# A hybrid encoder step on one core: squares and their parts issued earlier, values transposed once, the last attention units and a norm moved between weight pieces

## The chip, the core and the metric

The kernel runs on one core of one Trainium2 chip. The metric is the device time of one execution in microseconds (us). The kernel before was timed three times: 1239.25, 1239.58 and 1239.84 us, with the median at 1239.58. One execution was also recorded with the hardware profiler; all rows shown in this document are from such recordings.

## The reference

One layer of a streaming encoder works on 320 rows of width 2048 (256 of a new stream, 64 of a running one), in float32. What is computed, cut to what matters:

```python
z = rmsnorm(x, ln_g) @ w_in             # 2048 -> 1024 q, 128 k, 128 v, 1024 u, 1024 v_gate
q, k = rmsnorm(q, q_g), rmsnorm(k, k_g)  # per head of 64; 16 query heads, 2 key heads
a = sink_attention(q, k, v, bias, sinks) # chunks of 64 queries see up to 192 keys
s = gelu(u) * (W_s @ rmsnorm(gelu(v_gate)) + b)   # chunks of 128, chunk-causal
x = x + concat(rmsnorm(a), rmsnorm(s)) @ w_out
y = x + relu(rmsnorm(x) @ w_up)**2 @ w_down       # 2048 -> 8192 -> 2048
```

New keys, new values and the normalised gate rows of the running stream are returned too.

## The kernel before

All activations are held transposed: features lie on the partitions, and the 320 rows run along the free dimension. Every float32 weight is split into a rounded part and a remainder (`w_hi` on ScalarE, L115; `w_lo` on VectorE, L116), the activations likewise, and each product is the sum of three matmuls, hi times hi, hi times lo and lo times hi (L141). Weights come by the SP queue in pieces of 512 KB. A **piece** is four k-tiles by 256 output columns and gives 24 matmuls of 320 columns; a product over 2048 has four pieces. Three buffers each hold `w_hi` and `w_lo`, so a piece can be split while TensorE is up to three pieces behind.

The order of the products is: queries 0 together with keys and values in a first loop of twelve small steps (L237), which runs while x itself arrives; queries 1, 2 and 3; four products of the gate's v; four of u; then w_out, w_up and w_down. The first loop's steps append to `steps` the instructions that split that step's weights. x is normalised after the product: its squares (L288) are added up (L290 to L292), split into two parts (`two_parts`, L177 and L178), summed over the partitions by two matmuls with a constant matrix (L186, L187), and a reciprocal root `rx` is iterated on VectorE (L190 to L196). The evictions of the products multiply by `rx`.

Small matmuls are put between the pieces: `between_pieces` names, for each piece, a function to call when that piece has been issued; `narrow` is the list of such matmuls, and the next piece is ordered behind its last entry. What is put there: the norms (`rstd`), the sums of the queries' squares (`norm_q`, L323, whose result takes a way over ScalarE, two DMAs on the POOL queue, VectorE and POOL), the values' transposes (`values`, L349: six transposes in six windows of the 320 rows, copied by VectorE at L354), and the attention. `attend(i)` is a pipeline over ten units: it transposes the probabilities of unit i-2 into two PSUM banks called `misc` (L472), computes the scores of unit i (L420), and multiplies the transposed probabilities of unit i-3 with the values (L485); then come the softmax of unit i, the eviction of the attention output (L495, L497), and the copies of the transposed probabilities out of the two `misc` banks (L501). There are two `misc` banks in all, and `norm_q`, `rstd` and the row norm of the gate (`rows_norm`, L166 to L171) take one each for a while.

A scheduler decides at build time in which order the instructions stand on each engine; `issue_after(ins)` puts instructions of the block that are on the engine of `ins` behind it, and binds no other engine.

Of the kernel before, what the change touches and what calls it, by code (L numbers as in the profile page):

```python
# [15 lines left out]
P = 128  # L16
T = 320
# [3 lines left out]
KT = DM // P  # L21
# [9 lines left out]
def hymba_step_kernel(ctx: ExitStack, tc: tile.TileContext, i, o):  # L31
# [16 lines left out]
    def score_bank(p, name="s_ps"):  # L48
        return ps_sc.tile([P, 512], F32, name=f"{name}{p}", tag=f"s{p}")
# [50 lines left out]
    nc.vector.memset(hone[HD:P, 1:2], 1.0)  # L100


    loads, between, rests, steps, narrow, carry = [], [], [], [], [], []

    def load(out, in_):

# [15 lines left out]
    def products(w, k0, nk, c0, ps, rh, rl, deep=None, between_pieces={}, halves_behind={}):  # L122

        wv = w.rearrange("(kt p) n -> p kt n", p=P)
        behind = carry.pop() if carry else None
        steps.clear()
        for a in range(0, nk, 4):
            raw = (deep or wp).tile([P, 4, 256], F32, name="w_raw", tag="w_raw")  # L130
            hi, lo = w_tiles()
            load(raw, wv[:, k0 + a:k0 + a + 4, c0:c0 + 256])
            with tc.issue_after(halves_behind[a // 4]()) if a // 4 in halves_behind else nullcontext():
                high, low = halves(raw, hi, lo)
            tail = isinstance(ps, list) and a + 4 == nk
            for k, g in [(k, g) for g in range(2) for k in range(4)] if tail else [(k, g) for k in range(4) for g in range(2)]:
                kk = a + k
                for x, (w_, r_) in enumerate(((hi, rh), (hi, rl), (lo, rh))):
                    out = ps[g][:, 0:T] if isinstance(ps, list) else ps[:, g, 0:T]
                    with tc.issue_after(behind) if behind else nullcontext():  # L140
                        mm = nc.tensor.matmul(out=out, lhsT=w_[:, k, g * P:(g + 1) * P], rhs=r_(kk),  # L141
                                              start=(kk == 0 and x == 0), stop=(kk == nk - 1 and x == 2))
            steps.append((high, low, mm.ins))
            if a // 4 in between_pieces:
                with tc.issue_after(mm.ins):
                    between_pieces[a // 4]()
                    behind = narrow[-1]
                if a + 4 == nk:
                    carry.append(behind)
# [24 lines left out]
    def two_parts(acc):  # L174
        hl = sm.tile([P, 2, T], F32R, name="n_hl", tag="w2", bufs=4)
        hi, lo = hl[:, 0], hl[:, 1]
        nc.scalar.activation(out=hi, in_=acc, func=AF.Copy)  # L177
        rests.append(nc.vector.tensor_tensor(out=lo, in0=acc, in1=hi.bitcast(F32), op=ALU.subtract).ins)  # L178
        return hi, lo

    def rstd(acc, mean, eps, out):

# [101 lines left out]
    ssq2 = sm.tile([P, 2, T], F32, name="ssq2", tag="w2", bufs=4)  # L284
    for k in range(0, KT, 2):
        sq = sm.tile([P, 2, T], F32, name="sq2", tag="w2", bufs=4) if k else ssq2
        with tc.issue_after(steps[min(8 + k // 2, 11)][0]):
            nc.scalar.activation(out=sq, in_=xT[:, k:k + 2], func=AF.Square)  # L288
        if k:
            nc.vector.tensor_tensor(out=ssq2, in0=ssq2, in1=sq, op=ALU.add)  # L290
    ssq = sums("ssq")
    nc.vector.tensor_tensor(out=ssq, in0=ssq2[:, 0], in1=ssq2[:, 1], op=ALU.add)  # L292

    kv = sm.tile([P, 2, T], F32, name="kv", tag="w2", bufs=4)
    with tc.issue_after(steps[-1][0]):
        nc.scalar.activation(out=kv, in_=kv_ps[:, :, 0:T], func=AF.Copy)
    rk, rx = rstd_b("rk"), rstd_b("rx")

# [2 lines left out]
    def evict_q(g, q_ps):  # L301
        qg = qT[:, :, 2 * g:2 * g + 2]
        rx_b = rx.rearrange("p (b t) -> p b t", b=5)
        if g == 0:
            for a in range(2):
                rests.append(nc.vector.tensor_tensor(out=qg[:, :, a], in0=q_ps[a][:, 0:T].rearrange("p (b t) -> p b t", b=5),
                                                     in1=rx_b, op=ALU.mult).ins)
        else:
            nc.vector.tensor_tensor(out=qg.rearrange("p b a t -> p a b t"),
                                    in0=q_ps[:, :, 0:T].rearrange("p a (b t) -> p a b t", b=5),  # L310
                                    in1=rx_b[:, None].to_broadcast([P, 2, 5, 64]), op=ALU.mult)
        sq = sm.tile([P, 5, 2, 64], F32, name="qsq", tag="w2", bufs=4)
        nc.scalar.activation(out=sq, in_=qg, func=AF.Square)
        return sq

    q_dram = dram.tile([2, 2, 2, 2, T], F32, name="q_dram")
    r_at = lambda g, b, p: (g // 2) * 20 + p * 10 + (g % 2) * 5 + b

    def norm_q(h, sqs):

        st = misc()
        for c in range(4):
            mm = nc.tensor.matmul(out=st[c * 32:(c + 1) * 32, 0:T], lhsT=hone, rhs=sqs[c // 2][:, :, c % 2], start=True, stop=True)  # L323
        narrow.append(mm.ins)
        rows = sm.tile([P, T], F32, name="q_rows", tag="w1", bufs=3)
        nc.scalar.activation(out=rows, in_=st[:, 0:T], func=AF.Copy)
        for c in range(4):
            nc.gpsimd.dma_start(out=q_dram[h, c % 2, :, c // 2], in_=rows[c * 32:c * 32 + 2])
        r = at.tile([P, 20], F32, name="r_q", tag="r_q")
        for a in range(2):  # L330
            nc.gpsimd.dma_start(out=r[a * HD:(a + 1) * HD],
                                in_=q_dram[h, a].rearrange("p g (b t) -> t p (g b)", t=HD))
        nc.vector.tensor_scalar(out=r, in0=r, scalar1=HD * EPS, scalar2=None, op0=ALU.add)
        nc.gpsimd.tensor_tensor(out=rq[:, 20 * h:20 * h + 20], in0=r, in1=nhalf, op=ALU.pow)
# [6 lines left out]

        return [misc() if x < 2 else score_bank(3 - x, "g_ps") for x in range(skip, skip + n)]

    def values(*xs):
        for x, vps in zip(xs, [score_bank(1, "vps"), misc()] if len(xs) == 2 else banks(4)):
            t0 = (0, 64, 128, -64, 192, 256)[x]
            n = min(P, T - t0)
            with tc.issue_after(narrow[-1]):
                mm = nc.tensor.transpose(out=vps[0:n, 0:P], in_=kvx[:, 448 + t0:448 + t0 + n], identity=ident)  # L349
            narrow.append(mm.ins)  # L350
            for dst, r in (((v0, slice(0, P)), (w3, slice(HD, P))), ((v64, slice(0, P)),),
                           ((v128, slice(0, P)), (w2, slice(0, HD))), ((w2, slice(HD, P)),),
                           ((w3, slice(0, HD)), (vD, slice(HD, P))), ((w4, slice(0, HD)),))[x]:
                nc.vector.tensor_copy(out=dst[r], in_=vps[r, 0:P].rearrange("k (h d) -> k h d", h=2))  # L354


    q1_ps = product(w_in, 0, KT, 256, xh, xl, between_pieces={0: lambda: rstd(ssq, mean_dm, EPS, rx)},
                    halves_behind={2: lambda: rests[-1]})

    zk = kv[:, 0]  # L360
    nc.vector.tensor_tensor(out=zk, in0=zk, in1=rx, op=ALU.mult)
    nc.vector.tensor_tensor(out=vT, in0=kv[:, 1], in1=rx, op=ALU.mult)
    ksq = sums("ksq")
    nc.scalar.activation(out=ksq, in_=zk, func=AF.Square)
    q0_sq = evict_q(0, q0_ps)
    q0_out = rests[-1]
    q1_sq = []

    def first_norms():
        rstd(ksq, mean_hd, EPS, rk)  # L370
        q1_sq.append(evict_q(1, q1_ps))

    def keys():
        for dst, c in ((kn[:, 0:256], slice(0, 256)), (kn[:, 384:448], slice(256, 320))):
            nc.vector.scalar_tensor_tensor(out=dst, in0=zk[:, c], scalar=g_k, in1=rk[:, c], op0=ALU.mult, op1=ALU.mult)
        for h in range(2):
# [5 lines left out]
        nc.gpsimd.dma_start(out=o["ksT"], in_=kn[:, 384:448])  # L382
        nc.gpsimd.dma_start(out=o["vpT"], in_=vT[:, 128:256])
        nc.gpsimd.dma_start(out=o["vsT"], in_=vT[:, 256:320])
        values(0, 1)

    q2_ps = product(w_in, 0, KT, 512, xh, xl,
                    between_pieces={0: first_norms, 1: lambda: norm_q(0, (q0_sq, q1_sq[0])), 2: keys, 3: lambda: values(2, 3, 4, 5)},
                    halves_behind={1: lambda: q0_out})
    q2_sq = evict_q(2, q2_ps)  # L390


# [138 lines left out]
    gvs = at.tile([P, 8, HD], F32, name="gvs", bufs=1)  # L531
    for g in range(4):
        v_ps = product(w_in, 0, KT, 2304 + g * 256, xh, xl, between_pieces={
            1: lambda: attend(2 * g + 2), 2: lambda: norm_q(1, (q2_sq, q3_sq)) if g == 0 else None,
            3: lambda: attend(2 * g + 3)})
        gelu2(v_ps, gv[:, 2 * g:2 * g + 2])
        for a in range(2 * g, 2 * g + 2):
            add_square(acc_v, gv[:, a], a == 0)
            for dst, c in ((gv[:, a, 0:256], slice(0, 256)), (gvs[:, a], slice(256, T))):
                with tc.issue_after(ready[0]) if g == 3 else nullcontext():  # L540
                    nc.gpsimd.tensor_scalar(out=dst, in0=gv[:, a, c], scalar1=g_sv[:, a:a + 1], scalar2=None, op0=ALU.mult)
# [37 lines left out]
    def rows_norm():  # L579
# [2 lines left out]
    acc_s = sums("acc_s")  # L582
    parts_a, rm_a = [], rstd_b("rm_a")
    u_pieces = {
        0: {1: lambda: attend(10), 3: lambda: attend(11)},
        1: {1: lambda: (rows_norm(), attend(12), by_rows((0, 0))), 2: lambda: by_rows((1, 0), (0, 1), (1, 1), (2, 0)),
            3: lambda: spatial(0, 1, 2, 3)},
        2: {1: lambda: spatial(4, 5, 6, 7)},
        3: {1: lambda: rstd(tuple(parts_a), mean_1k, EPS, rm_a)}}
    gus = {}  # L590
# [159 lines left out]
```

## Time and profile before

| what | value |
|---|---|
| median of three runs | 1239.58 us |
| the profiled execution, its own time | 1239.04 us |
| its span, first to last instruction | 1237.3 us |
| TensorE matmuls busy | 1232.8 us (100%) |
| VectorE busy | 663.6 us (54%) |
| ScalarE busy | 492.0 us (40%) |
| POOL busy | 114.0 us (9%) |
| granted TensorE clock | 1.000 |

PE is TensorE's matmuls, PEld its weight loads, DVE is VectorE, ACT is ScalarE, SP the queue that issues the weights' DMAs. A row of the timeline gives start and duration in us, engine, source line, operation, what it writes and reads, and in brackets the idle time of that engine before it and what ended it. A row of the chain of waits gives start, duration, and the work that the end is traced back through; pieces of the same kind are merged with their count. Float32 transposes and scores are recorded as more than one matmul in some rows.

### The profile page before, as it was taken

How to read it: one execution, taken by the hardware profiler on the slowest of the kernel's cores; microseconds unless marked ns; L12 is line 12 of the kernel's file. 1: busy time of each engine (PE TensorE's matmuls, PEld its weight loads, DVE VectorE, ACT ScalarE, POOL GpSimd, SP SyncE). 2: the span in 40 equal slices, each digit the busy share in tenths (PEclk: the TensorE clock that was granted, in tenths of full speed). 3: DMA queues.
4: the chain of work that ended last, by engine and by line, in shares of the span. 5: the costliest groups of instructions: out<-in, count | busy, mean ns of one | idle time of the engine just before them, and what ended most of it. 6: DMA issues, size and time to landing. Idle time of an engine off the chain costs nothing.

```text
span 1237.3 us, 20626 instructions
## 1 busy us (share of the span) xinstructions
PE 1232.8 (100%) x8666; PEld 1225.0 (99%) x8666; DVE 663.6 (54%) x796; ACT 492.0 (40%) x652; POOL 114.0 (9%) x139
## 2 busy tenths in 40 slices
PE   9999999999999999999999999999999999999998
PEld 9999999999999999999999999999999999999998
DVE  7877778877864444444444444444444434444343
ACT  7446566435534432333434332344432333433321
POOL 3127454102200000000000000000000000000000
PEclk9999999999999999999999999999999999999999
DMA  9753346444555444454444444455444454445540
GB/s 282 226 148 104 104 138 195 153 154 141 151 152 153 153 147 145 152 154 149 146 149 153 154 150 143 151 154 152 147 147 151 154 151 144 150 152 164 172 161 33
DMA packets 187934, 188.03 MB, mean 152 GB/s; under 512 B 7616, under 2 KB 187376, under 8 KB 187840
## 3 DMA queue, kind: packets, MB, share of 16 engines
q1 hardware_dynamic: 186544, 185.48, 48.7%
q0 software_dynamic: 864, 0.98, 0.4%
q8 instruction: 68, 1.11, 0.4%
q10 hardware_dynamic: 432, 0.24, 0.1%
q14 instruction: 26, 0.21, 0.1%
HBM read 183.10 MB, written 3.35 MB: 151 GB/s over the span
## 4 chain that ended last, share of the span: by engine, by line
PE 99%; DVE 0%; issue 0%; ACT 0%; DVEq 0%
PE acc L141 93%; PE q_ps L237 1%; PE misc L141 1%; PE acc L237 1%; PE s_ps L420 1%; PE misc L472 0%; PE misc L83 0%; PE misc L485 0%; PE s_ps L485 0%; PE g_ps L566 0%; PE misc L566 0%; PE misc L553 0%; PE misc L323 0%; ACT s L449 0%; ACT w_hi L115 0%
## 5 line engine op out<-in xcount | busy, mean ns | idle before, releaser
L116 DVE TENSOR_TENSOR w_lo<-w_raw,w_hi 128x1024 fp32r<-128x1024 f32 x332 | 416.0, 1253 | 422.7 <-ACT w_hi L115 414.1
L115 ACT ACTIVATE w_hi<-w_raw 128x1024 fp32r<-128x1024 f32 x332 | 351.8, 1060 | 670.9 <-PE acc L141 646.7
L141 PE MATMUL acc<-H2H,w_lo 128*128 128x320 f32 x1024 | 316.4, 309 | 0.0
L141 PE MATMUL acc<-H2H,w_hi 128*128 128x320 f32 x1024 | 316.4, 309 | 0.0
L141 PE MATMUL acc<-H2L,w_hi 128*128 128x320 f32 x1024 | 316.4, 309 | 0.0
L141 PE MATMUL acc<-FH,w_hi 128*128 128x320 f32 x992 | 306.5, 309 | 0.0
L141 PE MATMUL acc<-FL,w_hi 128*128 128x320 f32 x992 | 306.5, 309 | 0.0
L141 PE MATMUL acc<-FH,w_lo 128*128 128x320 f32 x992 | 306.5, 309 | 0.0
L141 PEld LDWEIGHTS acc<-H2H,w_hi 128*128 128x128 f32 x1024 | 192.2, 188 | 0.0
L141 PEld LDWEIGHTS acc<-H2L,w_hi 128*128 128x128 f32 x1024 | 192.2, 188 | 0.0
L141 PEld LDWEIGHTS acc<-H2H,w_lo 128*128 128x128 f32 x1024 | 192.2, 188 | 0.0
L141 PEld LDWEIGHTS acc<-FH,w_hi 128*128 128x128 f32 x992 | 186.2, 188 | 0.0
L141 PEld LDWEIGHTS acc<-FL,w_hi 128*128 128x128 f32 x992 | 186.2, 188 | 0.0
L141 PEld LDWEIGHTS acc<-FH,w_lo 128*128 128x128 f32 x992 | 186.2, 188 | 0.0
L141 PE MATMUL acc<-XH,w_hi 128*128 128x320 f32 x352 | 110.7, 314 | 0.0
L141 PE MATMUL acc<-XH,w_lo 128*128 128x320 f32 x352 | 108.8, 309 | 0.0
L141 PE MATMUL acc<-XL,w_hi 128*128 128x320 f32 x352 | 108.7, 309 | 0.0
L141 PEld LDWEIGHTS acc<-XH,w_hi 128*128 128x128 f32 x352 | 66.1, 188 | 3.1 <-issue 3.0
L141 PEld LDWEIGHTS acc<-XL,w_hi 128*128 128x128 f32 x352 | 66.1, 188 | 0.0
L141 PEld LDWEIGHTS acc<-XH,w_lo 128*128 128x128 f32 x352 | 66.1, 188 | 0.0
L658 DVE SCALAR_TENSOR_TENSOR tf<-acc,r 128x640 f32<-128x640 f32 x32 | 26.4, 824 | 41.8 <-PE acc L141 41.8
L673 DVE TENSOR_TENSOR xT<-xT,acc 128x640 f32<-128x640 f32 x31 | 25.5, 821 | 41.8 <-PE acc L141 41.8
(227 smaller groups left out, 1086.3 us busy)
## 6 DMA issues: line engine op xcount, KB each, us to landing
w_raw<-in_w_up SPq DMA_DIRECT2D x128, 512.0 KB
w_raw<-in_w_down SPq DMA_DIRECT2D x128, 512.0 KB
w_raw<-in_w_in SPq DMA_DIRECT2D x44, 512.0 KB
w_raw<-in_w_out SPq DMA_DIRECT2D x32, 512.0 KB
w_first<-in_w_in SPq DMA_DIRECT2D x14, 256.0 KB
out_yT<-xT SPq DMA_DIRECT2D x7, 320.0 KB
xT<-in_xT SPq DMA_DIRECT2D x8, 160.0 KB
xT<-in_xT SPq DMA_DIRECT2D x4, 320.0 KB
```

Source lines behind the costliest of these rows:

```text
L115: return (pin(nc.scalar.activation(out=hi, in_=raw, func=AF.Copy)).ins, pin(nc.vector.tensor_tensor(out=lo, in0=raw, in1=hi.bitcast(F32), ...
L116: pin(nc.vector.tensor_tensor(out=lo, in0=raw, in1=hi.bitcast(F32), op=ALU.subtract)).ins)
L141: mm = nc.tensor.matmul(out=out, lhsT=w_[:, k, g * P:(g + 1) * P], rhs=r_(kk), start=(kk == 0 and x == 0), stop=(kk == nk - 1 and x == 2))
L237: mm = nc.tensor.matmul(out=ps[:, 0:T], lhsT=w_[:, j, k, g * P:(g + 1) * P], rhs=r_(a + k), start=(a + k == 0 and x == 0), stop=(a + k == ...
L420: mm = nc.tensor.matmul(out=s_ps[p][x * HD:(x + 1) * HD, j * nk:(j + 1) * nk], lhsT=qT[hs, blk_, a + x], rhs=kz[hs, kv, k0:k0 + nk], start ...
L658: nc.vector.scalar_tensor_tensor(out=t, in0=ps[:, :, 0:T], scalar=0.0, in1=r2[:, None, :].to_broadcast([P, 2, T]), op0=ALU.max, op1=ALU.mult)
L673: nc.vector.tensor_tensor(out=xT[:, a, c], in0=xT[:, a, c], in1=p, op=ALU.add)
```

## The change

There are three groups of edits.

1. The squares of x may be issued from the sixth step of the first loop on instead of the ninth. The two parts of x's sum are made right behind the sum, ahead of the eviction of keys and values; those of the keys' sum right behind it, ahead of the squares of queries 0. The splits of two weight pieces are ordered behind these parts, now on ScalarE as well as on VectorE.
2. `values` makes three transposes (rows 0 to 127, 128 to 255, 256 to 319) into one score bank, at piece 1 of queries 2, ahead of `norm_q(0)`. Ten copies on ScalarE, behind the eviction of `norm_q(0)`, put them at the places that the attention reads. The former calls, two transposes behind piece 2 and four behind piece 3, and their copies on VectorE are gone.
3. `norm_q(1)` moves from piece 2 of the gate's first v product to piece 1, behind `attend(2)`. `attend(10)` moves from piece 1 to piece 2 of u's first product, `attend(11)` from piece 3 of it to piece 0 of the second, and `rows_norm` from ahead of `attend(12)` to ahead of `attend(11)`.

```diff
     def two_parts(acc):
...
-        nc.scalar.activation(out=hi, in_=acc, func=AF.Copy)
+        firsts.append(nc.scalar.activation(out=hi, in_=acc, func=AF.Copy).ins)
...
+    def parts_of(acc):
+        hi, lo = two_parts(acc)
+        return hi, lo, firsts[-1], rests[-1]
...
-        with tc.issue_after(steps[min(8 + k // 2, 11)][0]):
+        with tc.issue_after(steps[min(5 + k // 2, 11)][0]):
             nc.scalar.activation(out=sq, in_=xT[:, k:k + 2], func=AF.Square)
...
+    parts_x = parts_of(ssq)
     kv = sm.tile([P, 2, T], F32, name="kv", tag="w2", bufs=4)
-    with tc.issue_after(steps[-1][0]):
+    with tc.issue_after(steps[-1][0]), tc.issue_after(parts_x[2]):
         nc.scalar.activation(out=kv, in_=kv_ps[:, :, 0:T], func=AF.Copy)
...
-        nc.scalar.activation(out=sq, in_=qg, func=AF.Square)
+        with tc.issue_after(firsts[-1]):
+            nc.scalar.activation(out=sq, in_=qg, func=AF.Square)
...
+    def values():
+        with tc.issue_after(narrow[-1]):
+            vps = score_bank(1, "vps").rearrange("k (x d) -> k x d", x=4)
+            for x, (t0, n) in enumerate(TT):
+                mm = nc.tensor.transpose(out=vps[0:n, x], in_=vT[:, t0:t0 + n], identity=ident)
+        narrow.append(mm.ins)
+        turned[:] = [vps]
+
+    def values_out():
+        vps = turned[0]
+        upper, lower, whole = slice(0, HD), slice(HD, P), slice(0, P)
+        for dst, to, x, of in ((v0, whole, 0, whole), (v128, whole, 1, whole), (w2, lower, 0, upper), (w2, upper, 1, upper),
+                               (v64, upper, 0, lower), (v64, lower, 1, upper), (w3, upper, 1, lower), (w3, lower, 0, lower),
+                               (vD, lower, 2, upper), (w4, upper, 2, upper)):
+            with tc.issue_after(turned[1]):
+                nc.scalar.activation(out=dst[to], in_=vps[of, x].rearrange("k (h d) -> k h d", h=2), func=AF.Copy)
...
-    q1_ps = product(w_in, 0, KT, 256, xh, xl, between_pieces={0: lambda: rstd(ssq, mean_dm, EPS, rx)},
-                    halves_behind={2: lambda: rests[-1]})
+    q1_ps = product(w_in, 0, KT, 256, xh, xl, between_pieces={0: lambda: rstd(parts_x[0:2], mean_dm, EPS, rx)},
+                    halves_behind={2: lambda: parts_x[2:4]})
...
     nc.scalar.activation(out=ksq, in_=zk, func=AF.Square)
+    parts_k = parts_of(ksq)
...
-        rstd(ksq, mean_hd, EPS, rk)
+        rstd(parts_k[0:2], mean_hd, EPS, rk)
...
-                    between_pieces={0: first_norms, 1: lambda: norm_q(0, (q0_sq, q1_sq[0])), 2: keys, 3: lambda: values(2, 3, 4, 5)},
-                    halves_behind={1: lambda: q0_out})
+                    between_pieces={0: first_norms, 1: lambda: (values(), norm_q(0, (q0_sq, q1_sq[0])), values_out()), 2: keys},
+                    halves_behind={1: lambda: (q0_out, *parts_k[2:4])})
...
-            1: lambda: attend(2 * g + 2), 2: lambda: norm_q(1, (q2_sq, q3_sq)) if g == 0 else None,
-            3: lambda: attend(2 * g + 3)})
+            1: lambda: (attend(2 * g + 2), norm_q(1, (q2_sq, q3_sq)) if g == 0 else None), 3: lambda: attend(2 * g + 3)})
...
-        0: {1: lambda: attend(10), 3: lambda: attend(11)},
-        1: {1: lambda: (rows_norm(), attend(12), by_rows((0, 0))), 2: lambda: by_rows((1, 0), (0, 1), (1, 1), (2, 0)),
-            3: lambda: spatial(0, 1, 2, 3)},
+        0: {2: lambda: attend(10)},
+        1: {0: lambda: (rows_norm(), attend(11)), 1: lambda: (attend(12), by_rows((0, 0))),
+            2: lambda: by_rows((1, 0), (0, 1), (1, 1), (2, 0)), 3: lambda: spatial(0, 1, 2, 3)},
```

In `norm_q`, the matmuls are now ordered behind the last of `narrow`, and its eviction is appended to `turned`. `keys` no longer calls `values(0, 1)`.

More of the change, by code (lines that the diff above doesn't have):

```diff
@@ L100, in hymba_step_kernel @@
     nc.vector.memset(hone[HD:P, 1:2], 1.0)
-    loads, between, rests, steps, narrow, carry = [], [], [], [], [], []
+    firsts, loads, between, rests, steps, narrow, carry = [], [], [], [], [], [], []
     def load(out, in_):
@@ L132, in products @@
             load(raw, wv[:, k0 + a:k0 + a + 4, c0:c0 + 256])
-            with tc.issue_after(halves_behind[a // 4]()) if a // 4 in halves_behind else nullcontext():
+            with ExitStack() as order:
+                for ins in halves_behind[a // 4]() if a // 4 in halves_behind else ():
+                    order.enter_context(tc.issue_after(ins))
                 high, low = halves(raw, hi, lo)
@@ L312, in evict_q @@
         sq = sm.tile([P, 5, 2, 64], F32, name="qsq", tag="w2", bufs=4)
-        nc.scalar.activation(out=sq, in_=qg, func=AF.Square)
+        with tc.issue_after(firsts[-1]):
+            nc.scalar.activation(out=sq, in_=qg, func=AF.Square)
         return sq
+    turned = []
     q_dram = dram.tile([2, 2, 2, 2, T], F32, name="q_dram")
@@ L321, in norm_q @@
         st = misc()
-        for c in range(4):
-            mm = nc.tensor.matmul(out=st[c * 32:(c + 1) * 32, 0:T], lhsT=hone, rhs=sqs[c // 2][:, :, c % 2], start=True, stop=True)
+        with tc.issue_after(narrow[-1]):
+            for c in range(4):
+                mm = nc.tensor.matmul(out=st[c * 32:(c + 1) * 32, 0:T], lhsT=hone, rhs=sqs[c // 2][:, :, c % 2], start=True,
+                                      stop=True)
         narrow.append(mm.ins)
         rows = sm.tile([P, T], F32, name="q_rows", tag="w1", bufs=3)
-        nc.scalar.activation(out=rows, in_=st[:, 0:T], func=AF.Copy)
+        turned.append(nc.scalar.activation(out=rows, in_=st[:, 0:T], func=AF.Copy).ins)
         for c in range(4):
@@ L342, in banks @@
         return [misc() if x < 2 else score_bank(3 - x, "g_ps") for x in range(skip, skip + n)]
[L344 to L354, printed above, removed]
-    q1_ps = product(w_in, 0, KT, 256, xh, xl, between_pieces={0: lambda: rstd(ssq, mean_dm, EPS, rx)},
-                    halves_behind={2: lambda: rests[-1]})
+    def values():
+        with tc.issue_after(narrow[-1]):
+            vps = score_bank(1, "vps").rearrange("k (x d) -> k x d", x=4)
[13 more added lines that the diff above has]
+                    halves_behind={2: lambda: parts_x[2:4]})
     zk = kv[:, 0]
@@ L384, in keys @@
         nc.gpsimd.dma_start(out=o["vsT"], in_=vT[:, 256:320])
-        values(0, 1)
     q2_ps = product(w_in, 0, KT, 512, xh, xl,
-                    between_pieces={0: first_norms, 1: lambda: norm_q(0, (q0_sq, q1_sq[0])), 2: keys, 3: lambda: values(2, 3, 4, 5)},
-                    halves_behind={1: lambda: q0_out})
+                    between_pieces={0: first_norms, 1: lambda: (values(), norm_q(0, (q0_sq, q1_sq[0])), values_out()), 2: keys},
+                    halves_behind={1: lambda: (q0_out, *parts_k[2:4])})
     q2_sq = evict_q(2, q2_ps)
```

## The prediction

> **What bounds the kernel now.** I read the page's head first, then a table by stages, and then the chain of waits in the stages that the change touches. The columns of the table are the stretch, its length, and the busy time and instructions of PE, weight loads, DVE, ACT and POOL, then clock, DMA share and GB/s.
>
> ```profile
> span 1237.3 us, 20626 instructions
> ```
> ```profile
> 0.00:33.50 33.50, 32.69 (x202) 31.46 (x203) 24.97 (x43) 25.64 (x42) 11.55 (x44) 1.00 0.94 279
> 33.50:63.70 30.20, 30.20 (x211) 29.48 (x211) 26.43 (x47) 12.35 (x16) 4.97 (x9) 1.00 0.73 212
> ...
> 150.00:178.00 28.00, 27.66 (x268) 26.31 (x261) 24.21 (x40) 17.65 (x39) 16.67 (x14) 1.00 0.39 114
> ...
> 200.00:1237.00 1037.00, 1033.99 (x7051) 1033.73 (x7049) 507.08 (x494) 377.92 (x408) 27.62 (x24) 1.00 0.48 150
> ```
>
> TensorE is the bound nearly everywhere, at full clock. From 33.5 to 63.7 us, where most of the edited lines act, PE is busy for all of 30.20 us, so DVE's 26.43 us there stand beside it and set nothing. Only 28.00 - 27.66 = 0.34 us of PE idleness is recorded between 150 and 178 us. The change therefore has two ways to act: it takes matmuls or switches out of TensorE's stream, and it removes or makes waits of the few small matmuls that stand between the pieces. Everything else is cover.
>
> **What is removed from TensorE's stream.** These are rows of the chain of waits (start, duration, work).
>
> ```profile
> 59.58 0.11 PE vps L349
> ...
> 59.79 3.52 PE acc L141 x24
> 63.31 0.22 PE misc L349 x2
> 63.53 0.22 PE g_ps L349 x2
> ...
> 86.47 0.81 PE s_ps L420 x16
> 87.28 3.71 PE acc L141 x24
> 90.99 0.68 PE misc L323 x8
> ```
>
> A value transpose costs 0.11 us, and the piece between two groups of them is a bare 3.52 us. Six become three: **-0.33 us**. A piece between the scores of `attend(2)` and `norm_q(1)` takes 3.71 us, 0.19 more than the bare one: leaving the small tiles and entering them again. With `norm_q(1)` (0.68 us either way) right behind `attend(2)`, one entry and one exit become a direct passage between two tile shapes, which no row shows. It costs between 0 and the same 0.19; I take half, **-0.10 us**.
>
> **The wait that goes.** Rows of the timeline of PE, then of DVE.
>
> ```profile
> 166.64 0.49 PE L472 MATMUL misc<-ident,s 128*128 128x128 f32 x3
> 167.47 0.52 PE L472 MATMUL misc<-ident,s 128*128 128x128 f32 x3 [0.34 <-DVE vnat L501]
> ```
> ```profile
> 163.57 2.43 DVE L116 TENSOR_TENSOR w_lo<-w_raw,w_hi 128x1024 fp32r<-128x1024 f32 x1 [0.29 <-ACT w_hi L115]
> 165.92 0.55 DVE L501 COPY kzv<-misc 128x384 f32<-128x384 f32 x1
> ...
> 166.78 0.55 DVE L501 COPY vnat<-misc 128x384 f32<-128x384 f32 x1
> ```
>
> `attend(11)` transposes into two `misc` banks; the second is free only when DVE has copied the second half of unit 8's probabilities, at 166.78 + 0.55 = 167.33. The second three could have followed after 3 x 0.11, at 166.97; they came at 167.47: 0.50 us of stall, of which the profile calls 0.34 idle, since the ends of matmuls are modelled. 0.14 us of it is the way from DVE's end to PE's start. After the change `attend(10)` comes one piece later (3.52 us), `attend(11)` more than a piece later too, while the DVE work ahead of these copies (the softmax of unit 9 and the splits) stays where it is. If DVE copies at 165.92 to 167.33 again, they end some 2 us ahead of `attend(11)`, which moves to 166.64 - 0.43 + 3.52 + 0.56 (the row sums ahead of it) = 170.3. **-0.50 us.**
>
> **The wait that comes.** `rows_norm` takes one `misc` bank, and `attend(11)`, right behind it, needs both. Before, `rows_norm` stood ahead of `attend(12)`, which transposes nothing and needs none. So one group of three transposes now waits until DVE has read the row sums (`r_rows`, L169); behind it on PE wait the 24 matmuls of that unit and then the whole next piece. PE's chain and DVE's timeline before:
>
> ```profile
> 176.03 0.56 PE misc L166 x6
> 176.60 0.82 PE s_ps L485 x24
> ```
> ```profile
> 171.04 1.17 DVE L206 SCALAR_TENSOR_TENSOR AL<-ao,cols,AH 128x320 fp32r<-128x320 f32 x1
> ...
> 172.73 1.01 DVE L501 COPY pt<-misc 128x384 f32<-128x384 f32 x2
> ...
> 178.25 0.15 DVE L169 TENSOR_SCALAR r_rows<-misc 128x3 f32<-128x3 f32 x1
> ```
>
> Lower bound: DVE is free, 0.15 us for the operation and 0.14 to PE are covered by the first three transposes (0.33): nothing. Upper bound: DVE takes it as late as before, 178.25 + 0.15 - 176.59 = 1.81 us behind the last row-sum matmul; 1.81 + 0.14 - 0.33 = 1.6 us. Between the ends I take half, **+0.80 us**: at about 170.3 us DVE is at work on splits of the attention output and of weights, operations of 0.5 to 1.2 us, so neither end is the natural one.
>
> ```profile
> 169.00 2.86 POOL L513 TENSOR_TENSOR acc_a<-acc_a,sq 128x320 f32<-128x320 f32 x2
> ```
>
> The 1.17 us row of AL lies beside this POOL row up to 171.86. The Trainium skill's page "SBUF — State Buffer", section "Who interferes with whom", says that a DVE instruction with two SBUF inputs contends with a GpSimd one that reads SBUF. By that rule whatever two-input split stands ahead of `r_rows` at 170 us is held until POOL is done, and the wait would lie near its upper bound rather than at half, the sum then at +0.67 us; this speaks against putting `rows_norm` here, and the trace's overlap agrees with it without proving it.
>
> `attend(12)` now follows `attend(11)` after one piece. It needs the copies of unit 9, which before ended 173.74 - 167.99 = 5.75 us after the transposes. The cover is 0.82 + 3.52 + 0.19 = 4.5 us. Lower bound 0, upper bound 5.75 + 0.14 - 4.5 = 1.4 us. I take 0, because the old delay was DVE's backlog up to 172.73, which belongs to the clock and not to the transposes; the new multiplication is due at 176.60 - 0.43 - 0.50, or 175.7 and what the first wait adds.
>
> **What is covered.** ACT's timeline, then two DVE rows and PE's first step of two k-tiles:
>
> ```profile
> 16.32 1.06 ACT L115 ACTIVATE w_hi<-w_first 128x1024 fp32r<-128x1024 f32 x1 [0.57 <-DMA w_first<-in_w_in]
> 17.28 0.72 ACT L288 ACTIVATE ssq<-xT 128x640 f32<-128x640 f32 x1
> ...
> 46.15 0.47 ACT L364 ACTIVATE ksq<-kv 128x320 f32<-128x320 f32 x1 [0.52 <-DVE kv L361]
> ...
> 56.04 0.42 ACT L326 ACTIVATE q_rows<-misc 128x320 f32<-128x320 f32 x1
> 59.47 1.06 ACT L115 ACTIVATE w_hi<-w_raw 128x1024 fp32r<-128x1024 f32 x1 [3.01 <-PE acc L141]
> ...
> 163.80 0.26 ACT L495 ACTIVATE ao<-misc 128x128 f32<-128x128 f32 x1
> ```
> ```profile
> 45.97 0.49 DVE L362 TENSOR_TENSOR kvx<-kv,rx 128x320 f32<-128x320 f32 x1
> 46.38 0.88 DVE L306 TENSOR_TENSOR qT<-q_ps,rx 128x320 f32<-128x320 f32 x2
> ```
> ```profile
> 19.23 0.75 PE L237 MATMUL q_ps<-XH,w_hi 128*128 128x320 f32 x4
> ```
>
> *Squares.* Three squares of 0.72 us can stand ahead of this `w_hi`: 2.16 us, of which 0.57 fill its DMA wait, so it ends at up to 17.38 + 1.59 = 18.97, against PE's use at 19.23. Cost 0; if the idle time is not met, 0.3 us. They gain nothing: PE reaches the sum's matmuls when the first piece of queries 1 is through, whatever is ready.
>
> *Parts of the keys' sum.* The split of queries 2's piece 1 now waits on ACT behind `ksq` (46.15) and one copy of like length, and on DVE behind the remainder: `w_hi` ends near 48.2 and `w_lo` near 49.5. PE wants that piece after `first_norms`; four bare pieces, 14.1 us, and 0.3 us of sums lie behind the first sums at about 37.3, so at 51.7. Two us of cover, cost 0.
>
> *Values.* vT is there at 46.46, long before the transposes at 55, and the bank of queries 0 is drained by 47.3. Ten ACT copies at 0.26 us or less are at most 2.6 us, in ACT's wait of 3.01 us; that `w_hi` is for a piece more than two pieces ahead, 7 us of cover. DVE loses its copies beside a dense PE. No DMA is added or removed; `norm_q(1)`'s six POOL DMAs are issued about one piece earlier, and what they serve, units 5 to 9, is not due for over 15 us.
>
> **The sum.** -0.33 - 0.10 - 0.50 + 0.80 = -0.13 us on the profiled execution: 1237.3 to 1237.2 of span, 1239.04 to 1238.9 of its own time, which lies 0.54 us below the median. The forecast for the median is 1239.58 - 0.13, rounded to **1239.4 us**. Changes below 0.2% (2.5 us) are what a measurement of this kernel cannot tell from none.
>
> **The rivals.**
>
> *The row sums are read at once.* DVE picks `r_rows` as its next instruction. For it: its operation is 0.15 us and its program order is ahead of u's second product. Against it: it stood behind two longer ones before. -0.93 us: 1238.65.
>
> *Both new waits at full price.* `r_rows` and then the copies of unit 9 stay as late relative to PE as before: -0.93 + 1.6 + 1.4 = +2.1 us, 1241.7. For it: both delays have their rows. Against it: when PE waits 1.6 us, DVE gains them for the copies.
>
> *Slower: `norm_q(1)` is shut out of its bank.* It needs a third `misc` behind `attend(2)`'s two, so DVE must have copied one of them when the scores are through.
>
> ```profile
> 86.39 0.29 DVE L501 COPY kzv<-misc 128x128 f32<-128x128 f32 x1 [0.62 <-PE misc L472]
> ...
> 107.96 0.54 DVE L501 COPY kzv<-misc 128x384 f32<-128x384 f32 x1
> ```
> ```profile
> 104.08 0.66 PE misc L472 x6
> ```
>
> In `attend(2)` DVE stood idle and copied at 86.39 to 86.68, 0.6 us ahead of the end of the scores at 87.28, so there is no wait if that order stays. But one `attend` later in the pipeline the first copy ended at 108.50, 4.42 us after its transposes began. The cover from the first transpose is 0.22 + 0.81 = 1.03 us; with that delay PE stalls 4.42 + 0.14 - 1.03 = 3.5 us, and the time is 1239.45 + 3.5 = 1242.95, slower by 0.27%. It decides from a copy that ends 0.9 us behind the first transpose.
>
> *It does not do what it says.* The copies of unit 8 are planned behind other work again, the 0.50 us stall stays and the new one is added: 1239.95.
>
> **How the numbers follow.** The forecast (row sums read after 0.3 to 1.3 us) 0.50; read at once 0.22; both waits 0.15; the old stall stays 0.06; `norm_q(1)` shut out 0.07. The range goes from 1238.4, below the second case by the spread of the three runs, to 1241.0, part of the way to both waits. More than 0.2% faster would need 2.5 us out of a stream in which I find 0.93: 0.02. More than 0.2% slower is the shut-out case and a little of the rest: 0.06. Within: 0.92.
>
> **What would show it.** Three L349 rows instead of six on PE, in one bank, ahead of L323 near 55 us; a piece of 3.7 us at most behind `norm_q(1)` and none ahead of it; no idle time of PE ahead of the L323 rows near 87 us; an L472 row that waits for `r_rows` near 170.5 us, by 0 to 1.6 us; L485 rows of `attend(12)` without a wait. The prediction is wrong if PE shows a wait of over 1 us anywhere in the first 64 us, or if its dense stretch behind 200 us changes by more than 0.5 us.

## The result, and the profile after

The changed kernel takes 1243.73 us (median of seven executions, 1242.58 to 1244.83) against 1239.58 us before (1239.25 to 1240.74): 4.15 us more, a ratio of 1.0031 with a 95% interval of 1.0022 to 1.0040. The forecast was 1239.4 us with a range to 1241.0. The profiled execution took 1242.89 us, which is 3.85 us above that of before.

The table by stages of the changed kernel, whose span is 1241.1 us (the columns are those of the table of before):

```profile
150.00:178.00 28.00, 25.63 (x206) 24.35 (x203) 25.18 (x41) 16.36 (x36) 19.28 (x15) 0.94 0.47 133
...
200.00:1237.00 1037.00, 1037.00 (x7077) 1037.00 (x7077) 509.99 (x498) 380.43 (x413) 30.57 (x27) 1.00 0.48 150
```

Most of the change lies in the stretch from 150 to 178 us: PE idles for 28.00 - 25.63 = 2.37 us of it where it idled for 0.34, and the mean granted clock is 0.94 where it was 1.00. Behind 200 us nothing differs (PE's 1033.99 us there before and 1037.00 now differ only because the row ends at 1237 us, when PE had been through for 3 us before and is still at work now). One landmark shows it, the gate's first spatial product in the chain of waits, before and then after:

```profile
196.04 0.44 PE misc L566 x4
```
```profile
199.88 0.45 PE misc L581 x4
```

It comes 3.84 us later, and from it to the end of the span there are 1041.3 us before (1237.3 - 196.04) and 1041.2 after. So all of the loss lies ahead of 200 us.

The early edits did what was forecast. The chain of waits, before (one row) and after the change:

```profile
95.38 0.44 PE misc L472 x4
```
```profile
54.96 0.33 PE vps L359 x3
55.29 0.68 PE misc L333 x8
55.96 14.28 PE acc L143 x96
...
85.93 0.81 PE s_ps L436 x16
86.74 0.68 PE misc L333 x8
...
94.65 0.44 PE misc L488 x4
```

There are three value transposes in place of six, and then four pieces with nothing between them (a transpose is one row of the recording, while the eight score matmuls of a unit are sixteen). `norm_q(1)` (the second L333 row) stands right behind the scores of `attend(2)`, and no bank is waited for. From these scores to the transposes of `attend(3)` it took 95.38 - 86.47 = 8.91 us before and takes 94.65 - 85.93 = 8.72 us now, for the same work in another order: all of the 0.19 us is saved, so the direct passage from the scores (64 x 64 tiles) to these sums (128 x 32) is free. At the scores of `attend(9)` PE is 0.72 us ahead; the timelines of PE, before and after:

```profile
149.51 0.88 PE L420 MATMUL s_ps<-kzv,qT 64*64 64x192 f32 x16
```
```profile
148.79 0.88 PE L436 MATMUL s_ps<-kzv,qT 64*64 64x192 f32 x16
```

0.33 of it are the transposes and 0.19 the passage; the other 0.20 lies ahead of the values, in how soon the first loop ended. That is no gain of the change: in the kernels below that share all the early edits, the same scores start anywhere from 148.72 to 149.41 us.

Then comes the stall. PE's timeline, DVE's and POOL's, after:

```profile
169.42 0.72 PE L168 MATMUL misc<-inv_1k,acc_v 128*128 128x1 f32 x6
170.00 0.53 PE L488 MATMUL misc<-ident,s 128*128 128x128 f32 x3
172.89 0.90 PE L488 MATMUL misc<-ident,s 128*128 128x128 f32 x3 [2.37 <-DVE r_rows L171]
```
```profile
169.53 1.77 DVE L116 TENSOR_TENSOR w_lo<-w_raw,w_hi 128x1024 fp32r<-128x1024 f32 x1
171.22 1.15 DVE L212 SCALAR_TENSOR_TENSOR AL<-ao,cols,AH 128x320 fp32r<-128x320 f32 x1
172.29 0.48 DVE L537 TENSOR_SCALAR gc<-gc 128x640 f32<-128x640 f32 x1
172.69 0.15 DVE L171 TENSOR_SCALAR r_rows<-misc 128x3 f32<-128x3 f32 x1
```
```profile
169.36 2.66 POOL L529 TENSOR_TENSOR acc_a<-acc_a,sq 128x320 f32<-128x320 f32 x2
```

The second three transposes of `attend(11)` could have started at 170.00 + 3 x 0.11 = 170.33; they started at 172.89, 2.56 us later, when DVE had read the row sums. The sums were ready by 170.1; ahead of `r_rows` stood a weight remainder, a split of the attention output and one step of the gelu.

Two more things show in these rows. The second three transposes take 0.90 us, the first three 0.53. The table by stages of the clock says why:

```profile
172.50:173.00 0.50, 0.11 (x1) 0.11 (x2) 0.50 (x3) 0.00 (x0) 0.15 (x1) 0.66 0.77 111
173.00:176.00 3.00, 3.00 (x30) 2.34 (x31) 2.71 (x2) 0.60 (x1) 3.00 (x2) 0.50 0.65 187
176.00:176.50 0.50, 0.50 (x5) 0.50 (x4) 0.33 (x1) 0.47 (x3) 0.50 (x2) 0.92 1.02 354
```

From about 172.7 to 176.1 us TensorE was granted half of its clock (0.66 and 0.92 are the shares of the first and last half microsecond). If all of PE's work slowed in that measure, this would cost 3.0 x 0.5 + 0.5 x 0.08 us and a little of the first slice, about 1.6 us; the first experiment below measures 1.42. And behind the next piece the chain of waits has an order of work that the kernel before did not have (that kernel's rows first; the multiplications ahead of them, at 176.60, are shown in the prediction):

```profile
177.41 0.59 PE misc L553 x4
...
181.51 0.87 PE misc L553 x8
```
```profile
179.38 0.36 PE s_ps L501 x2
179.74 0.37 PE misc L568 x2
180.11 0.36 PE s_ps L501 x2
180.47 0.37 PE misc L568 x2
180.83 0.15 PE acc L143
180.98 0.80 PE s_ps L501 x20
...
185.36 0.66 PE misc L568 x6
```

The multiplications of `attend(12)` (64 x 64 tiles) and the transposes by rows (L568, 128 x 128) alternate, since the scheduler's order binds the one to the other by nothing. From the first multiplication to the second group of transposes it took 181.51 - 176.60 = 4.91 us before and takes 185.36 - 179.38 = 5.98 us now.

### The profile page after: what moved, and what is told of

Its sections match the earlier page's. It is cut to its first block, busy times and chain, and to the rows that moved or that the text cites. A ratio compares the mean times of both kernels' runs of the same rounds, so it can differ in the third digit from the quotient of the medians.

```text
span 1241.1 us, 20619 instructions
## 1 busy us (share of the span) xinstructions
PE 1234.7 (99%) x8663; PEld 1226.1 (99%) x8663; DVE 662.7 (53%) x787; ACT 494.3 (40%) x662; POOL 113.4 (9%) x139
## 4 chain that ended last, share of the span: by engine, by line
PE 99%; DVE 0%; issue 0%; ACT 0%; DVEq 0%; ACTq 0%
PE acc L143 93%; PE q_ps L243 1%; PE misc L143 1%; PE acc L243 1%; PE s_ps L436 1%; PE misc L488 0%; PE misc L83 0%; PE s_ps L501 0%; PE misc L501 0%; PE g_ps L581 0%; PE misc L581 0%; PE misc L568 0%; ACT s L465 0%; PE misc L333 0%; DVE w_lo L116 0%
```

## The experiments

Each kernel was timed beside the kernel before, whose median was 1239.57, 1239.81, 1239.75 and 1239.61 us in the four sittings. Intervals are at 95%.

**The late moves alone.** The kernel before, with only the table `u_pieces` of the changed one.

```diff
-        0: {1: lambda: attend(10), 3: lambda: attend(11)},
-        1: {1: lambda: (rows_norm(), attend(12), by_rows((0, 0))), ...
+        0: {2: lambda: attend(10)},
+        1: {0: lambda: (rows_norm(), attend(11)), 1: lambda: (attend(12), by_rows((0, 0))), ...
```

> The kernel before, with only the last attention units and the row sums at their new places. Theory A (the row sums' bank, then TensorE's clock, then mixed tile shapes): the old wait of 0.5 us at the copies of unit 8 goes, a wait of about 2.5 us for the row sums comes, the granted clock is half for about 3.4 us behind it (1.7 us), and the mixed matmuls of attend(12) and the rows' transposes cost 0.9 us; 4.6 us slower than before, near 1244.2, with the clock below 1.0 in the 2 us slices behind 172 us. Rival B (the wait comes from VectorE's order having been shifted by the early parts and the values): without these the row sums are read within 1 us, no half clock, within 0.7 us of before.

Measured: 1243.56 us (1242.44 to 1245.00), ratio 1.0032 (1.0020 to 1.0044). The whole slowdown is here. PE's timeline:

```profile
173.83 0.55 PE L472 MATMUL misc<-ident,s 128*128 128x128 f32 x3 [1.82 <-DVE r_rows L169]
```

The same wait, 1.82 us of idling against 2.37, without any early edit; these did not put DVE's work in a worse order.

This profiled execution kept the full clock, so it gives the price of the half clock. The start of `attend(12)` in its chain of waits:

```profile
178.90 0.36 PE s_ps L485 x2
```

From the second three transposes to `attend(12)` it takes 178.90 - 173.83 = 5.07 us, the changed kernel 179.38 - 172.89 = 6.49 us for the same work: the half clock cost 1.42 us. Only one of the six executions had a mean clock of 1.000.

**Everything but the late moves.** The changed kernel with the old `u_pieces`, the reverse of the diff above.

> The changed kernel with the last attention units and the row sums at their old places: squares, values and norm_q(1) stay changed. Theory A: three transposes less (0.33), one passage of tile shapes less (0.19) and 0.2 from the first loop as the two profiles show; 0.7 us faster than before, near 1238.9, and the old wait of 0.5 us at attend(11) still there. Rival B: some of the loss stays here, 1 us or more above before.

Measured: 1239.32 us (1239.06 to 1239.72), ratio 0.9997 (0.9988 to 1.0007). Half a microsecond was saved early on and does not arrive. PE's timeline shows where it goes:

```profile
158.50 0.52 PE L488 MATMUL misc<-ident,s 128*128 128x128 f32 x3 [0.61 <-DVE pt L517]
```

`attend(10)`, which had no wait before, now waits for DVE's copies as well, and `attend(11)` idles for 0.34 us as before. DVE did not become earlier, so a TensorE that is earlier waits for it. All ten executions had a mean clock of 1.000.

**The earlier squares and parts alone.** The kernel before, with the first group of edits only.

```diff
-        with tc.issue_after(steps[min(8 + k // 2, 11)][0]):
+        with tc.issue_after(steps[min(5 + k // 2, 11)][0]):
...
+    parts_x = parts_of(ssq)
...
+    parts_k = parts_of(ksq)
```

> The kernel before with only the earlier squares and the earlier parts of x's and the keys' sums. All theories: TensorE waits for none of them, so the sum of matmuls starts at the same place in its stream; no change, 1239.6, within 0.3 us. If the squares push the splits of a step past TensorE's use, up to 0.3 us slower.

Measured: 1239.30 us (1239.00 to 1240.18), ratio 0.9997 (0.9988 to 1.0006). No difference that stands clear of the noise: TensorE was not waiting for these sums.

**`rows_norm` back to its old place.**

```diff
-        1: {0: lambda: (rows_norm(), attend(11)), 1: lambda: (attend(12), by_rows((0, 0))),
+        1: {0: lambda: attend(11), 1: lambda: (rows_norm(), attend(12), by_rows((0, 0))),
```

> The changed kernel with only the row sums back ahead of attend(12); the attention units stay late. Theory A: no wait for the row sums, clock full throughout, no mixed tile shapes, old wait gone: 1.2 us faster than before, near 1238.4. Rival C (the late units are the cost: attend(12) one piece behind attend(11) waits for the copies of unit 9): a wait of 1 us or more stays at attend(12), and the time is above 1239.6.

Measured: 1242.52 us (1240.93 to 1243.79), ratio 1.0023 (1.0014 to 1.0033). The wait for `r_rows` is gone, the alternation too, and another wait has come. PE's timeline and DVE's:

```profile
176.89 0.83 PE L168 MATMUL misc<-inv_1k,acc_v 128*128 128x1 f32 x6 [1.51 <-DVE pt L517]
```
```profile
174.53 1.84 DVE L212 SCALAR_TENSOR_TENSOR AL<-ao,cols,AH 128x320 fp32r<-128x320 f32 x1
176.29 0.55 DVE L517 COPY pt<-misc 128x384 f32<-128x384 f32 x1
```

Now the banks are full of unit 9's probabilities, whose copies stand behind the splits. Here too the clock went to half, from about 179.55 to 182.96 us.

**The transposes by rows kept behind `attend(12)`.**

```diff
-                mm = nc.tensor.transpose(out=vps[:, a * P:(a + 1) * P], in_=cols, identity=ident)
+                with tc.issue_after(narrow[-1]):
+                    mm = nc.tensor.transpose(out=vps[:, a * P:(a + 1) * P], in_=cols, identity=ident)
```

> The changed kernel with the rows' transposes ordered behind the matmuls of attend(12), so that the tile shapes no longer alternate there. Theory A: the wait and the half clock stay, only about 0.9 us goes: near 1242.8. If alternating shapes cost nothing, as changed: 1243.7.

Measured: 1242.80 us (1241.23 to 1243.65), ratio 1.0023 (1.0013 to 1.0034). The chain of waits:

```profile
179.85 0.82 PE s_ps L501 x24
180.67 0.59 PE misc L569 x4
...
184.77 0.87 PE misc L569 x8
```

The same work takes 184.77 - 179.85 = 4.92 us here and 185.36 - 179.38 = 5.98 us in the changed kernel: alternating cost 1.06 us, and the medians differ by 0.93. The wait for `r_rows` (2.55 us of idling) and the half clock stayed.

The eight executions of this kernel fall into groups by the mean granted clock: 1241.23 and 1241.32 at 1.000; 1242.31 and 1242.53 at 0.999 and 0.998; four of 1243.08 to 1243.65 at 0.997. One stretch of 3.4 us at half clock takes 1.7 of 1241 us, or 0.0014, from the mean. So the middle group fits one such stretch, which its profiled execution shows, and the last fits two; no execution at 0.997 was profiled, so the two are an inference. The groups lie 1.1 us apart, less than the 1.42 that a half clock takes from the stream; the run with a filled wait shows why.

**Filling the wait, first attempt.** Sixteen matmuls, whose results nobody reads, into free columns of the row sums' bank.

```diff
+FILL = 16
...
+        for _ in range(FILL):
+            with tc.issue_after(narrow[-1]):
+                mm = nc.tensor.matmul(out=st[:, 128:448], lhsT=mean_1k, rhs=XH[:, 0], start=True, stop=True)
+            narrow.append(mm.ins)
```

> The changed kernel with 16 matmuls of 320 columns between the row sums and attend(11), into columns of the row sums' bank that nothing reads: 16 x 0.147 = 2.35 us of work in place of most of the 2.4 us wait; the rows' transposes come out behind attend(12) here too, as in the run with them ordered. If the half clock behind the wait is TensorE's answer to being idle, the clock stays at 1.0 in all runs and the time sits at 1241.3 with little scatter, where the ordered run scattered from 1241.2 to 1243.7. If the half clock has another cause, scatter and median stay as in the ordered run, 1242.8.

Measured: 1245.31 us (1243.44 to 1246.23), ratio 1.0043 (1.0028 to 1.0058). It failed as a filler: the bank's reader had to be through first, and the matmuls waited themselves. PE's timeline:

```profile
173.30 4.14 PE L175 MATMUL misc<-XH,mean_1k 128*128 128x320 f32 x16 [2.88 <-DVE r_rows L172]
```

**Filling the wait, in an unused score bank.** The ordering edit, and the same sixteen matmuls into a spare bank, between the row sums and `attend(11)`.

```diff
-        1: {0: lambda: (rows_norm(), attend(11)), ...
+        1: {0: lambda: (rows_norm(), fill(), attend(11)), ...
```

> The changed kernel with the rows' transposes ordered and the same 16 matmuls (2.35 us) between the row sums and attend(11), now into a score bank that holds nothing, so that they need not wait for the row sums' bank. They add nothing to the path as long as the row sums are read later than they end. If the half clock is TensorE's answer to idling, all runs have a mean clock of 1.0 and lie near 1241.4, without the spread of the ordered run (1241.2 to 1243.7, median 1242.8). If it has another cause, the spread and the median stay.

Measured: 1241.23 us (1240.99 to 1241.73), ratio 1.0012 (1.0003 to 1.0022). PE's timeline, and the clock by stages:

```profile
170.62 2.59 PE L602 MATMUL spare<-XH,mean_1k 128*128 128x320 f32 x16
```
```profile
173.00:176.00 3.00, 2.96 (x39) 2.38 (x38) 3.00 (x5) 0.00 (x0) 2.46 (x1) 1.00 0.71 184
```

TensorE loses the same 2.6 us to work of no use, but it does not idle, and its clock stays at 1.00; nine of ten executions have a mean clock of 1.000, where two of eight had without the filling. The median is 1.57 us lower and equals the two undisturbed executions of `rows_ordered`. So it is the idling that lowers the clock, and this costs about 1.6 us in the median. One reserve: the filled kernel ran on another chip than `rows_ordered`, and no unfilled kernel with this wait ran there. On the chip of `rows_ordered`, though, the clock stayed at 1.000 in all ten executions without the late moves.

Filling does not save all of the 1.42 us, since a TensorE at full clock meets the next wait. The chain of waits ahead of `attend(12)`:

```profile
174.95 3.23 PE acc L143 x21
...
179.10 0.87 PE s_ps L501 x20
```

The piece from 174.95 on would end at 174.95 + 3.71 = 178.66; the twenty L501 matmuls start at 179.10, 0.44 us late, behind DVE's copy of `pt`. In the changed kernel the half clock hid this wait.

**The same filling without the ordering edit.**

```diff
-                with tc.issue_after(narrow[-1]):
-                    mm = nc.tensor.transpose(...)
+                mm = nc.tensor.transpose(...)
```

> The changed kernel with the sixteen spare matmuls ahead of attend(11), and without the edit that keeps attend(12) and the transposes by rows apart. With the clock kept up by the spare matmuls, as in the same kernel with that edit (1241.23 us), this measures the alternation of the two tile shapes by itself. Theory (alternation costs about 1.3 us, from the rows 179.31 to 181.72 us of the changed kernel): 1242.5 us, L501 and L568 rows in turns, few executions with a lowered clock. Rival (what looked like the price of alternating was the scatter of the clock): 1241.2 us, within 0.3 us of the kernel with the edit.

Measured: 1241.33 us (1241.14 to 1241.97), ratio 1.0014 (1.0005 to 1.0023). The number is the rival's, but the run does not decide: with the filling in place, the scheduler put the two kinds of matmuls apart by itself, as PE's timeline shows.

```profile
178.49 1.38 PE L501 MATMUL s_ps<-pt,kzv 64*64 64x128 f32 x24
```

It repeats the run before it. The price of alternating rests on the rows of the changed kernel, of `rows_ordered` and of the kernel before.

**POOL's additions left out.** The ordering edit, and the three additions of squares of the attention output in u's second product left out; the norm of the attention output, and all that depends on it, is then another one.

```diff
-                add_square(acc_a, ao[:, a], a == 0)
+                if g == 2 or a == 0:
+                    add_square(acc_a, ao[:, a], a == 0)
+                else:
+                    sq = sm.tile([P, T], F32, name="sq", tag="w1", bufs=3)
+                    nc.scalar.activation(out=sq, in_=ao[:, a], func=AF.Square)
```

> The changed kernel with the rows' transposes ordered, and POOL's three additions of squares of the attention output during the second u product left out (the sum of squares of units' output lacks three of eight terms, so the attention norm is another). Same VectorE order. If POOL's reads lengthen VectorE's two-input splits, those at 169.5 and 171.2 us fall from 1.77 and 1.15 us to 1.22 and 0.55, the row sums are read 1.1 us sooner and the wait falls to 1.4 us: near 1240.2 without the half clock. If not, the rows keep their durations and the time stays at 1242.8.

Measured: 1241.69 us (1240.28 to 1242.09), ratio 1.0012 (1.0003 to 1.0022). DVE's timeline, then PE's:

```profile
169.92 1.21 DVE L116 TENSOR_TENSOR w_lo<-w_raw,w_hi 128x1024 fp32r<-128x1024 f32 x1
171.05 0.54 DVE L212 SCALAR_TENSOR_TENSOR AL<-ao,cols,AH 128x320 fp32r<-128x320 f32 x1
```
```profile
172.12 0.55 PE L488 MATMUL misc<-ident,s 128*128 128x128 f32 x3 [1.43 <-DVE r_rows L171]
```

In the same order on DVE, the remainder falls from 1.77 to 1.21 us and the split from 1.15 to 0.54, together 1.17 us; the wait falls from 2.55 to 1.43. A little under half of the wait is DVE being held up by POOL; the rest is the queue in front of `r_rows`.

**`r_rows` ahead of the split on DVE.** The ordering edit, and the splits of piece 2 of u's second product ordered behind `r_rows`.

```diff
-        nc.vector.tensor_scalar(out=r, in0=st[:, 0:3], ...)
+        read.append(nc.vector.tensor_scalar(out=r, in0=st[:, 0:3], ...).ins)
...
-        u_ps = product(..., between_pieces=u_pieces.get(g, {}))
+        u_ps = product(..., between_pieces=u_pieces.get(g, {}), halves_behind={2: lambda: read} if g == 1 else {})
```

> The changed kernel with the rows' transposes ordered, and the split of the second u product's piece 2 ordered behind the reading of the row sums on VectorE. Theory A (the wait is only the place of that reading in VectorE's order): its wait falls from 2.5 to 0.7 us, nothing takes its place, 1239.5. Theory D (VectorE has more to do between 163 and 178 us than it can, so whatever stands last there waits): the copies of unit 9 still end near 177.5 and attend(12), due at 175.7, waits some 1.5 to 2 us for them; 1240.5 to 1242.

Measured: 1241.83 us (1241.46 to 1243.84), ratio 1.0018 (1.0009 to 1.0027). PE's timeline:

```profile
172.10 0.55 PE L488 MATMUL misc<-ident,s 128*128 128x128 f32 x3 [1.32 <-DVE r_rows L171]
179.26 0.87 PE L501 MATMUL s_ps<-pt,kzv 64*64 64x128 f32 x20 [0.21 <-DVE pt L517]
```

Half of the wait is gone, and `attend(12)` begins to wait for the copies of unit 9. The clock still went to half, from about 173.2 to 176.6 us.

**The splits of the attention output one product later.** The ordering edit, and:

```diff
-        for x, a in enumerate(((), (0, 1, 2), (3, 4, 5), (6, 7))[g]):
-            high, low, _ = steps[x + 1]
+        for x, a in enumerate(((), (), (0, 1, 2, 3), (4, 5, 6, 7))[g]):
+            high, low, _ = steps[min(x + 1, 3)]
```

> The changed kernel with the rows' transposes ordered and the splits of the attention output moved one product of u later, so that 3.65 us of VectorE work (0.68 + 1.15 + 1.82) leaves the stretch from 163 to 178 us. Theory D: the row sums are read some 1.8 us sooner, the wait falls to about 0.8 us, the clock stays at 1.0, attend(12) waits for nothing: 1239.2, or below. If the splits were not what VectorE was late with, above 1241.

Measured: 1243.01 us (1241.61 to 1243.55), ratio 1.0026 (1.0015 to 1.0037). PE's timeline and DVE's:

```profile
171.33 0.55 PE L488 MATMUL misc<-ident,s 128*128 128x128 f32 x3 [0.28 <-DVE r_rows L171]
178.60 0.53 PE L501 MATMUL s_ps<-pt,kzv 64*64 64x128 f32 x4 [2.19 <-DVE pt L517]
```
```profile
176.43 1.56 DVE L540 SCALAR_TENSOR_TENSOR gu<-gc,z 128x640 f32<-128x640 f32 x1 [3.08 <-ACT gc L539]
177.91 0.55 DVE L517 COPY pt<-misc 128x384 f32<-128x384 f32 x1
```

This is the clearest of the runs. The wait for `r_rows` is almost gone, and 2.4 us of waiting (2.19 and, one group of matmuls later, 0.24) stand one unit later. DVE had nothing to do for 3.08 us, but the copies stood behind `gu`, the last step of the gelu of u's first product, which goes from DVE over ScalarE and POOL back to DVE. DVE does not step over it. No cover is left when `attend(12)` follows `attend(11)` after one piece.

**The copies ahead of the softmax.** To keep the early gain: the changed kernel with the old `u_pieces`, the copies of the probabilities ahead of the softmax on DVE, and a split of u's second product behind those of unit 8.

```diff
+        if t is not None:
+            for p in range(2):
+                ...
+                copied = nc.vector.tensor_copy(out=pts[t % 2][p][:, c], in_=bank[p][:, c]).ins
         if i < 10:
             softmax(i, s_ps)
...
-                nc.vector.tensor_copy(out=pts[t % 2][p][:, c], in_=bank[p][:, c])
```

> Squares, values and norm_q(1) as changed, the last attention units at their old places, and two edits on VectorE's order: each unit's copies out of the misc banks stand ahead of the next softmax, and the split of the second u product's first piece stands behind the copies of unit 8. Theory D (what the early parts save is given back where TensorE waits for these copies, 0.77 us at attend(10) and 0.50 at attend(11) in the run without the late units): both waits go, nothing else changes, and the time is 1239.3 - 0.77 - 0.50 = 1238.0, 0.12% faster than before. If the waits are set by something else than the order on VectorE, 1239.3.

Measured: 1240.03 us (1239.30 to 1240.30), ratio 1.0001 (0.9992 to 1.0010). Missed. The wait at `attend(11)` is gone, the one at `attend(10)` is longer. PE's timeline and DVE's:

```profile
159.13 0.52 PE L488 MATMUL misc<-ident,s 128*128 128x128 f32 x3 [0.97 <-DVE ao L519]
```
```profile
158.25 0.54 DVE L509 COPY pt<-misc 128x384 f32<-128x384 f32 x1
```

The bank is not free with the copy: it also holds an attention output, whose addition now comes behind the copy, and the copy itself was no earlier (158.79 at its end, 158.08 in the kernel before). No version was found that is faster than the kernel before by more than its interval.

## Why the prediction was wrong

The forecast was a sum of -0.13 us; here are its terms and what the profiled executions show.

| step | forecast, us | measured, us |
|---|---|---|
| six value transposes become three | -0.33 | -0.33 |
| `norm_q(1)` behind `attend(2)` | -0.10 (0 to -0.19) | -0.19 |
| old stall at `attend(11)` | -0.50 | -0.50 |
| new wait for `r_rows` | +0.80 (0 to +1.6) | +2.56 |
| `attend(12)` waits for unit 9 | 0 (0 to +1.4) | 0, but see below |
| half clock | not in the sum | +1.42 |
| alternating tile shapes | not in the sum | +1.06 |
| start of the stretch (varies between executions) | not in the sum | -0.20 |
| sum | -0.13 | +3.82 (landmark: +3.84) |

The steps that took work out of TensorE's stream were right, and so were those costed at nothing: no other new PE wait appears in the first 200 us. `norm_q(1)` was not shut out of its bank. In the kernel without the late moves, though, these gains fall to a wait at `attend(10)`, which the sum had not asked about: it took a gain early in the stream as a gain at the end. One reading was off without harm: between the copies' end at 167.33 and 170.3 us there were 3.0 us and not "some 2"; in the changed kernel the copies ended at 168.88, 1.1 us ahead of `attend(11)`.

**The step that failed** is "Between the ends I take half, +0.80". The mechanism was right and its place too; the size was off (2.56 us), and the upper bound of 1.6 us with it. That bound moved the delay of the old place (1.81 us behind the row sums) to a new one. But the delay was not a property of `r_rows`. It was whatever DVE had queued at that time. The rows of before that the prediction shows beside this very bound have the 1.17 us AL row at 171.04 and copies at 172.73, so DVE was seen to be at work around 171 to 173.7 us. A reading of that time, rather than of the old wait, would have put `r_rows` behind the AL row, at 172.2 us or later; it came at 172.69.

The rule of the Trainium skill, "SBUF — State Buffer", section "Who interferes with whom", that a DVE instruction with two SBUF inputs contends with a GpSimd one that reads SBUF, was the better guide of the two, and the run without POOL's additions agrees: 1.12 us less wait. The +0.67 us that it was given in the prediction was too little all the same, for it was held to the same bound.

**What the sum had no term for.** TensorE answers the wait by half a clock for 3.4 us (shown by filling the wait, with the reserve given there), and the moved matmuls met others of another tile shape in an order that nothing fixed (shown by the rows with and without the ordering edit). Together they cost 1.42 + 1.06 = 2.48 us, as much as the wait. No rival had them either: the one that came nearest in time, both waits at 1241.7 us, has the second wait, which was not there.

**The wait at `attend(12)`** was forecast as none, and there is none, but only because PE came late. Where the first wait is taken away, the second comes: 1.51 us with `rows_norm` moved back, 2.4 us with the splits moved, over the bound of 1.4. At full clock behind a filled wait there are 0.44 us of it. The sentence against the rival of both waits, that DVE gains what PE waits, held; what it did not see is that the copies of unit 9 end between 177.5 and 179.3 us in the profiled execution of every kernel with the late units but the first filling, whatever PE waited for before, so that a TensorE which comes earlier waits there instead.

A change below 2.5 us was called one that a measurement of this kernel cannot tell from none; the intervals above reach 1.1 to 1.5 us to either side, and 1.9 us for the kernel with four executions.

What stays open: why some executions lose the clock not at all, some once and some, it seems, twice; and some tenths of the median, which is 0.84 us above the profiled execution of the changed kernel.

## What to carry to other kernels

When a small matmul is moved, read the timeline of the engine that frees its buffer at the new time, instruction by instruction; a delay seen at the old place says nothing of the new one, and taking one wait away can only show the next when both stand in the same in-order queue. A wait of TensorE of 1.3 us or more should be priced with a chance of half a clock behind it, here 1.4 us more per drop where no other wait hides it. And work of different tile shapes that is brought together needs an order written out between them.

## What the runs showed of the hardware

**An idle of 1.3 to 2.9 us can halve TensorE's clock for 3.4 us.** The half clock begins between 0.2 us before PE is back at work and 2.7 us after: idle to 172.9 and half clock from 172.7 in the changed kernel; idle to 172.1 and half clock from about 173.2 with `r_rows` ahead; idle to 176.9 and half clock from about 179.55 with `rows_norm` back. The profiled executions of the late moves alone and without POOL's additions idled for 1.8 and 1.4 us without a drop. The Trainium skill, "TensorE: Matmul & The Clock Gate", section "What's actually happening", has the half clock after at least one idle window of some 3.4 us, and a window that runs freely. The length of 3.4 us agrees with these traces. That a shorter gap suffices is measured here and goes beyond that rule; a free-running window would fit that the same wait costs nothing in some executions, but no run here shows its phase.

**Changing the tile shape has no one price.** Directly from 64 x 64 scores to the sums of `norm_q` it was free. In alternation, four more changes between the 64 x 64 and 128 x 128 shapes cost 1.06 us, 0.27 each, where leaving the small tiles and entering them again cost 0.19 around a whole piece. That it is the shape and not something else in the alternating order that costs this, no run separates.
